# Attention scores as one product for two heads, and later first transposes in the gated feed-forward blocks

## The chip, the cores and the metric

One NeuronCore of a Trainium2 chip runs the whole program in one launch. The metric is device time in microseconds (us), the median of several runs; lower is better. TensorE is written PE, its weight loads PEld, VectorE DVE, ScalarE ACT, GpSimdE POOL, the queue that issues loads SP.

## The reference

256 tokens of width 1024 go through sixteen sublayers in float32. Eight are gated feed-forward blocks, two are squared-ReLU feed-forward blocks, the other six are mixers. Four of the mixers hold attention with heads of 64:

```python
# dsa: 8 indexer heads pick keys, then 16 heads share one key and value head
logits = jnp.einsum('bthd,bsd->bths', qi_b, ki32)
score = jnp.einsum('bth,bths->bts', wi_b, jax.nn.relu(logits))
s = jnp.einsum('bthd,btkd->bhtk', q_b, k_sel) * scale
# diff: two causal softmaxes per head, 8 heads
s = jnp.einsum('btchd,bschd->bchts', q_b, k32) * scale
a = p[:, 0] - lam_val * p[:, 1]
# pool and moba: 4 heads against 256 memory rows, no mask; moba also 12 causal heads
s = jnp.einsum('bshd,bmhd->bhsm', q, k) * (HEAD_DIM ** -0.5)
# gated feed-forward
return (jax.nn.silu(gate) * up) @ w_out
```

## The kernel before

Weights come from HBM in chunks of 1 MB (128 x 2048), through SP. Each float32 chunk is split by ACT (`hi`, L306) and DVE (`lo`, L311) into two reduced-precision parts, and each large product is issued three times (hi by hi, hi by lo, lo by hi; L528 to L530 in the gated blocks, L557 to L559 and L539 to L541 in the mixers, L598 for the down products). `take` hands the chunks out in the order of a plan that `_ffn_plan` and `_U_ORDER` write. The order of instructions on each engine is set by a scheduler that goes by priorities and by when buffers come free; each engine then runs its own list strictly in order.

**A gated feed-forward block** (`ffn`). Blocks 0 to 3 of 128 hidden columns are computed by `first` with tokens on the rows, so their results (`hts`, L728) must be turned by eight transposes (`turn`, L736) and split (L673, L674) before a down product can use them. From block 4 on the products (`u_products`, 48 for a block) give the hidden columns on the rows directly. `turn` is queued behind the 20th product of block 4, the fifth block. The first down chunk, V0, follows block 4, V1 follows block 5, and from there one down chunk follows every two blocks. `more` issues a share of the modulation sums (L1104, DVE) with each chunk in the blocks that carry them.

**Attention scores** (`softmax_pair`, and the indexer in `dsa`). Two heads of 64 are stacked on the 128 rows of `qT` and `kT`. Each head is a product of its own over its 64 rows: for query half m (128 queries) and head i, `lhsT=qT[h, 128m:...]`, `rhs=kT[h, :n]`, with n = 128 keys for m = 0 and 256 for m = 1 where the mask is causal, else 256 for both. Head i has PSUM bank a0 or a1, both halves in one bank. One such product is two MATMUL records in the trace. DVE then adds the mask and takes the row maximum (L1244, or L1246 where there is no mask), ACT takes the exponential (L1255), PE transposes (L1265) and multiplies by the values (L1280). There are 22 causal calls of `softmax_pair` (8 in dsa, 8 in diff, 6 in moba), 4 calls without mask (2 in pool, 2 in moba), and 4 pairs of indexer heads (L1351) in the form of a causal call. Keys are turned by `turn4` into the PSUM tile `tr` and copied by one ACT instruction (`to_heads`, L1202).

**Small tiles.** `square` writes a bf16 tile `junk` (one buffer), `turned` an f32 tile `turn` (two buffers). POOL does little: the root of the norms (L422, L423, in `rstd`) and a few fills.

Of the kernel before, what the change touches and what calls it, by code (L numbers as in the profile page):

```python
# [11 lines left out]
F32 = mybir.dt.float32  # L12
# [32 lines left out]
def _ffn_plan(tag, nf):  # L45
    ng = nf // 2
    out = []
    for g in range(ng):
        out += _w(tag, 2 * g, 2 * g + 1) if g < 2 else [("U", tag, 2 * g), ("U", tag, 2 * g + 1)]
        if g == 2:  # L50
            out.insert(-1, ("V", tag, 0))
        if 1 < g < ng - 3:
            out.append(("V", tag, g - 1))
    return out + [("V", tag, g) for g in range(ng - 4, ng)]
# [214 lines left out]
class _K:  # L269
# [143 lines left out]

    def square(self, src, st, n):

        j = self.tmp.tile([128, 512], BF16, name="junk")
        self.nc.scalar.activation(j, src, AF.Square, scale=1.0 / 32, accum_out=st[:, n:n + 1])  # L417

    def rstd(self, st):
# [237 lines left out]
    def turned(self, pp):  # L657

        nc = self.nc
        o = self.ps("tr")  # L660
        for m in range(2):
            t = self.tmp.tile([128, 256], F32, name="turn", bufs=2)
            nc.scalar.activation(t, pp[m], AF.Copy)
            for b in range(2):
                nc.tensor.transpose(o[:, 256 * b + 128 * m:256 * b + 128 * m + 128], t[:, 128 * b:128 * b + 128], self.ident)
        return o
# [11 lines left out]
    def ffn(self, s, act):  # L678
        nc, tc = self.nc, self.tc
        nf = 22  # L680
        with tc.tile_pool(name="hp_" + s, bufs=2) as hp:
# [59 lines left out]
            for g in range(2, 11):  # L741
                for f in (2 * g, 2 * g + 1):
                    w = self.take(("U", s, f))
                    more()
                    p = self.ps()
                    products = self.u_products(w, act, p, 1 if s[0] == "g" and f == nf - 1 else 2)
                    if f == 4:
                        self.issue(products, 20, turn)
                    else:
                        self.issue(products)  # L750
                    hidden(f, p)
                    if f == 4:
                        acc = self.new_acc()
                    if f == 4 or (f % 2 and g < 8):
                        j = 0 if f == 4 else g - 1
                        w = self.take(("V", s, j))
                        more()
                        for m in range(2):
                            self.down(m, acc[m], w, hs(j), (128, 128), j == 0, False)
# [441 lines left out]
    def to_heads(self, src, out):  # L1201
        self.nc.scalar.activation(out, self.turn4(src), AF.Copy)  # L1202

    def split_pair(self, on, oact, b0):

        pv = self.turn4(on)
        h = oact[0][:, b0:b0 + 2]
        self.nc.scalar.activation(h, pv, AF.Copy)
        self.nc.vector.tensor_tensor(oact[1][:, b0:b0 + 2], pv, h.bitcast(F32), op=OP.subtract)
# [13 lines left out]
    def softmax_pair(self, pool, qT, kT, mask, causal=True, qs=None):  # L1223


        nc = self.nc
        mx = self.tiny.tile([128, 4], F32, name="mx")
        sums = self.tiny.tile([128, 4], F32, name="sums")
        e = pool.tile([128, 2, 2, S], F32, name="e", bufs=self.ebufs)
        ns = [128 if causal else 256, 256]  # L1230
        scale = 0.125 if qs is None else 1.0
        p = [self.ps("a0"), self.ps("a1")]
        for m in range(2):
            for i in range(2):
                h = slice(64 * i, 64 * i + 64)
                o = 256 * m
                nc.tensor.matmul(p[i][:, o:o + ns[m]], lhsT=qT[h, 128 * m:128 * m + 128], rhs=kT[h, :ns[m]], start=True, stop=True)  # L1237
        for i in range(2):
            for m in range(2):
                c = 2 * m + i  # L1240
                n = ns[m]
                pi = p[i][:, 256 * m:256 * m + n]
# [72 lines left out]
    def dsa(self, act):  # L1315
        nc, tc = self.nc, self.tc
        with tc.tile_pool(name="ds", bufs=2) as dp:
# [5 lines left out]
            kk = dp.tile([128, 2, S], F32, name="kk", bufs=1)  # L1323
# [6 lines left out]
            nc.scalar.activation(kk, p.rearrange("p (j t) -> p j t", j=2), AF.Copy)  # L1330
# [11 lines left out]
            for j in range(2):  # L1342
                qT = heads(p4[1 + j])
                for b in range(2):
                    p = [self.ps("a0"), self.ps("a1")]
                    r = dp.tile([128, 2, 2, S], F32, name="e", bufs=self.ebufs)
                    for m in range(2):
                        n = 128 * (m + 1)
                        for i in range(2):
                            h = slice(64 * i, 64 * i + 64)  # L1350
                            nc.tensor.matmul(p[i][:, 256 * m:256 * m + n], lhsT=qT[h, b, 128 * m:128 * m + 128], rhs=kk[h, 1, :n],  # L1351
                                             start=True, stop=True)
                        for i in range(2):
                            nc.scalar.activation(r[:, m, i, :n], p[i][:, 256 * m:256 * m + n], AF.Relu)
# [35 lines left out]
    def diff(self, act):  # L1390
        nc, tc = self.nc, self.tc
        lam_init = 0.8 - 0.6 * math.exp(-0.3)
        with tc.tile_pool(name="df", bufs=2) as dp:
# [17 lines left out]

            chunks = lambda i: self.vprojs("diff", _U_ORDER["diff"][i], act)

            def heads(pp, name):
                q = self.evac(dp, pp, "q")
                self.rope(q.rearrange("p m (h d) -> p m h d", h=4), 4, self.rope2, 16, dp)
                qT = dp.tile([128, 2, S], F32, name=name)
                self.to_heads(q, qT)
                return qT
# [109 lines left out]
    def mem_kv(self):  # L1529

        nc = self.nc
        l, kv, pool, mact = self.mem
        kT = kv.tile([128, 2, S], F32, name="memk")
        v = kv.tile([128, 2, 256], F32, name="memv")
        k = pool.tile([128, 2, 256], F32, name="memkk")
# [7 lines left out]
        return k, kT, v  # L1543

    def mem_keys(self, k, kT):
        self.to_heads(k, kT)
        self.mem_inner.close()

    def mem_query(self, l, pool, pp, bufs=2):
        qs = self.head_scales(pool, pp, 0.125)  # L1550
# [10 lines left out]

    def pool(self, act):
        nc, tc = self.nc, self.tc
        k, kT, v = self.mem_kv()
        p4 = self.first("pool", _U_ORDER["pool"], act)
        self.mem_keys(k, kT)
        with tc.tile_pool(name="po", bufs=2) as pp:
            self.rows_ahead("pool")
            psc = [self.tmp.tile([128, 512], F32, name="upd", bufs=2) for _ in range(2)]
            nc.sync.dma_start(psc[0], self.a["pscale"][:, :512].to_broadcast([128, 512]))  # L1570
# [45 lines left out]

    def moba(self, act):
        nc, tc = self.nc, self.tc
        km, kTm, vm = self.mem_kv()
        p4 = self.first("moba", _U_ORDER["moba"][:2], act)  # L1620
        self.mem_keys(km, kTm)
        self.rows_ahead("moba")
        with tc.tile_pool(name="mb", bufs=2) as mp:
            r3 = self.tmp.tile([128, D], F32, name="xn", bufs=1)[:, :256].rearrange("p (a d) -> p a d", a=4)
            nc.sync.dma_start(r3, self.a["k_rope3"].rearrange("p (a d) -> p a d", a=4))
            tabs = {}
# [18 lines left out]
                return x, qs  # L1645

            def turned(xs, name):
                t = mp.tile([128, 2, S], F32, name=name)
                self.to_heads(xs[0], t)
                return t if xs[1] is None else (t, xs[1])  # L1650

            key = lambda pp: turned(key_x(pp), "kT")
            query = lambda pp: turned(query_x(pp), "qT")
# [108 lines left out]
```

## Time and profile before

| what | us |
|---|---|
| median of 3 runs | 2673.6 (2661.34 to 2678.39) |
| the profiled execution | 2675.0 |
| its span, first to last instruction | 2672.9 |
| PE busy | 2630.4 (98%) |
| DVE busy | 1938.7 (73%) |
| ACT busy | 1378.1 (52%) |
| POOL busy | 105.3 (4%) |

The profiled execution is 1.4 us above the median; 2.1 us of it lie outside the span. The end of a matmul is modelled in the trace, so the busy time of PE counts its pipeline's tail, and the distance between starts tells more than the duration.

### The profile page before, as it was taken

To read this page: it belongs to the slowest core of one execution; us is meant where nothing else is said; L and a number is where in the kernel's file an instruction comes from. 1 tells how busy PE (TensorE), PEld (TensorE's weight loads), DVE (VectorE), ACT (ScalarE), POOL (GpSimd) and SP (SyncE) were. 2 spreads that over 40 slices of the span, in tenths; PEclk is the share of its full clock that TensorE was granted. 3 is DMA by queue.
4 is the path that set the end of the run, shared out by engine and by line. 5 is a ranking of instruction groups with operands and counts; after the bars stand their busy time and mean duration, and the time that the engine had idled before them with its cause. 6 is when DMAs were issued, how large, how long until landed. Compare 5 with 4: busy or idle time off the path is not lost.

```text
span 2672.9 us, 43146 instructions
## 1 busy us (share of the span) xinstructions
PE 2630.4 (98%) x15984; PEld 2312.8 (87%) x15984; DVE 1938.7 (73%) x5196; ACT 1378.1 (52%) x3054; POOL 105.3 (4%) x200
## 2 busy tenths in 40 slices
PE   8999999999999999999999999999999999999999
PEld 7998789989988899899779989977899788977898
DVE  7858887587578875985868778667855776577764
ACT  5545454454554544645665454456644655465543
POOL 0004200000000000000000000000100000000000
PEclk9999999999999999999999999999999899999999
DMA  8844166476424675784538668653554545542452
GB/s 317 303 158 158 71 251 244 168 302 242 165 107 176 259 279 186 283 308 163 184 140 303 257 232 328 221 192 127 205 189 174 184 144 203 187 170 95 179 185 94
DMA packets 91156, 543.60 MB, mean 203 GB/s; under 512 B 10541, under 2 KB 11581, under 8 KB 38082
## 3 DMA queue, kind: packets, MB, share of 16 engines
q1 hardware_dynamic: 90946, 540.85, 55.1%
q8 instruction: 125, 2.05, 0.3%
q14 instruction: 85, 0.70, 0.1%
HBM read 539.69 MB, written 1.13 MB: 202 GB/s over the span
## 4 chain that ended last, share of the span: by engine, by line
PE 56%; issue 35%; DVE 5%; ACT 2%; POOL 1%; DMA 1%; SPq 0%; POOLq 0%; ACTq 0%
PE a L598 20%; PE ps L528 8%; PE ps L530 8%; PE ps L529 8%; PE a L557 2%; PE a L559 2%; PE a L558 2%; DVE y L856 2%; DVE lo L311 1%; PE a L1237 1%; PE tr L479 1%; POOL ry L423 1%; PE ps L558 1%; PE ps L557 1%; PE ps L559 1%
## 5 line engine op out<-in xcount | busy, mean ns | idle before, releaser
L311 DVE TENSOR_TENSOR lo<-raw,hi 128x256 fp32r<-128x256 f32 (+1 forms) x2964 | 1160.3, 450 | 409.2 <-ACT hi L306 408.8
L306 ACT ACTIVATE hi<-raw 128x512 fp32r<-128x512 f32 x1652 | 946.8, 624 | 792.5 <-issue 271.7
L528 PE MATMUL ps<-xh,hi 128*128 128x256 f32 x2784 | 789.3, 284 | 0.0
L530 PE MATMUL ps<-xh,lo 128*128 128x256 f32 x2784 | 789.0, 283 | 0.0
L529 PE MATMUL ps<-xl,hi 128*128 128x256 f32 x2784 | 788.4, 283 | 0.0
L529 PEld LDWEIGHTS ps<-xl,hi 128*128 128x128 f32 x2784 | 533.3, 192 | 4.1
L528 PEld LDWEIGHTS ps<-xh,hi 128*128 128x128 f32 x2784 | 533.2, 192 | 3.9
L530 PEld LDWEIGHTS ps<-xh,lo 128*128 128x128 f32 x2784 | 533.6, 192 | 0.2
L598 PE MATMUL a<-hi,hh 128*128 128x512 f32 x960 | 309.6, 396 | 0.0
L598 PE MATMUL a<-hi,hl 128*128 128x512 f32 x960 | 309.2, 396 | 0.0
L598 PE MATMUL a<-lo,hh 128*128 128x512 f32 x960 | 309.2, 396 | 0.0
L598 PEld LDWEIGHTS a<-lo,hh 128*128 128x128 f32 x960 | 179.9, 188 | 43.7
L598 PEld LDWEIGHTS a<-hi,hl 128*128 128x128 f32 x960 | 179.9, 187 | 43.5
L557 PE MATMUL a<-hi,xh 128*128 128x512 f32 x512 | 202.0, 396 | 3.4 <-ACT xh L487 1.8
L598 PEld LDWEIGHTS a<-hi,hh 128*128 128x128 f32 x960 | 173.9, 188 | 35.6 <-ACT hh L673 0.2
L559 PE MATMUL a<-hi,xl 128*128 128x512 f32 x512 | 202.4, 396 | 1.0 <-DVE xl L488 1.0
L558 PE MATMUL a<-lo,xh 128*128 128x512 f32 x512 | 200.7, 392 | 0.3 <-DVE lo L311 0.3
L1104 DVE SCALAR_TENSOR_TENSOR adaj<-adaw,cond 128x1024 bf16<-128x1024 f32 x144 | 175.8, 1221 | 34.5 <-DMA adaw<-in_ada 33.7
L557 PEld LDWEIGHTS a<-hi,xh 128*128 128x128 f32 x512 | 97.0, 189 | 26.4 <-ACT xh L492 5.2
L559 PEld LDWEIGHTS a<-hi,xl 128*128 128x128 f32 x512 | 96.6, 189 | 25.4 <-DVE xl L488 4.0
L558 PEld LDWEIGHTS a<-lo,xh 128*128 128x128 f32 x512 | 96.9, 189 | 20.6 <-DVE lo L311 0.6
L442 DVE TENSOR_TENSOR upd<-a,pg 128x512 f32<-128x512 f32 x48 | 32.9, 688 | 75.0 <-ACT junk L417 75.0
(355 smaller groups left out, 2755.7 us busy)
## 6 DMA issues: line engine op xcount, KB each, us to landing
raw<-in_wall SPq DMA_DIRECT2D x413, 1024.0 KB, 4.8
adaw<-in_ada SPq DMA_DIRECT2D x144, 512.0 KB, 6.5
G<-in_rows SPq DMA_DIRECT2D x16, 512.0 KB, 5.3
pg<-in_rows SPq DMA_DIRECT2D x12, 512.0 KB, 4.6
xn<-modd SPq DMA_DIRECT2D x12, 512.0 KB, 3.3
cond<-condd SPq DMA_DIRECT2D x7, 512.0 KB, 5.7
memt<-in_mem SPq DMA_DIRECT2D x4, 512.0 KB, 3.2
x<-in_x SPq DMA_DIRECT2D x2, 512.0 KB, 5.8
```

The costliest lines, as they stand in the source:

```text
L306: self.nc.scalar.activation(h[:, c], r[:, c], AF.Copy)
L311: self.nc.vector.tensor_tensor(l[:, c], r[:, c], h[:, c].bitcast(F32), op=OP.subtract)
L442: nc.vector.tensor_tensor(t, acc[n], pg[:, s], op=OP.mult)
L528: yield self.nc.tensor.matmul(o, lhsT=wh[:, c], rhs=xh[:, k, :], start=(k == 0), stop=False)
L529: yield self.nc.tensor.matmul(o, lhsT=wh[:, c], rhs=xl[:, k, :], start=False, stop=False)
L530: yield self.nc.tensor.matmul(o, lhsT=wl[:, c], rhs=xh[:, k, :], start=False, stop=(k == 7))
L557: yield self.nc.tensor.matmul(p, lhsT=xh[:, k, t], rhs=wh[:, c], start=(k == 0), stop=False)
L558: yield self.nc.tensor.matmul(p, lhsT=xh[:, k, t], rhs=wl[:, c], start=False, stop=False)
L559: yield self.nc.tensor.matmul(p, lhsT=xl[:, k, t], rhs=wh[:, c], start=False, stop=(k == 7))
L598: mm = lambda l, r, i, st, sp: nc.tensor.matmul(acc[i], lhsT=l[:k, t], rhs=r[:k, 1024 * b + 512 * i:1024 * b + 512 * i + 512], start=st, s ...
L856: nc.vector.scalar_tensor_tensor(c, hp[:, j, t:t + S], w(t), c, op0=OP.mult, op1=OP.add)
L1104: self.nc.vector.scalar_tensor_tensor(junk, self.ada_w.pop(n), 1.0, self.cond, op0=OP.mult, op1=OP.mult, accum_out=self.mods[k][:, c:c + 1])
```

## The change

Keys get a tile twice as wide, [128, 2, 2, 256] (`key_tile`): for each pair of heads it holds the keys of head 0 on rows 0 to 63 with zeros below, and those of head 1 on rows 64 to 127 with zeros above. POOL fills the zeros once for each tile (two fills of 64 x 512), and ACT copies keys in by two instructions of 64 rows. A score product then takes all 128 rows and gives both heads side by side, 2 x 128 or 2 x 256 columns, one query half in each of the banks a0 and a1. Six such tiles exist: one in dsa, two used in turn in diff, one in pool, two in moba (one of them first for the memory's keys). The indexer's ReLU becomes one ACT instruction for both heads. In `ffn`, `turn` comes behind the 40th product of block 4, V0 and V1 both follow block 5, and block 4 no longer calls `more`. `junk` gets two buffers, and `turned` uses it. The memory's raw keys move to another pool.

```diff
@@ _ffn_plan
         if g == 2:
-            out.insert(-1, ("V", tag, 0))
+            out.append(("V", tag, 0))
@@ ffn
-                    more()
+                    if f > 4:
+                        more()
...
                     if f == 4:
-                        self.issue(products, 20, turn)
+                        self.issue(products, 40, turn)
...
-                    if f == 4 or (f % 2 and g < 8):
-                        j = 0 if f == 4 else g - 1
+                    for j in ((0, 1) if f == 5 else (g - 1,) if f % 2 and g < 8 else ()):
@@ new
+    def key_tile(self, pool, name, tag=None):
+        t = pool.tile([128, 2, 2, S], F32, name=name, bufs=1)
+        self.nc.gpsimd.memset(t[64:, :, 0], 0.0)
+        self.nc.gpsimd.memset(t[:64, :, 1], 0.0)
+        return t
+    def to_keys(self, pv, t):
+        self.nc.scalar.activation(t[:64, :, 0], pv[:64], AF.Copy)
+        self.nc.scalar.activation(t[64:, :, 1], pv[64:], AF.Copy)
+        return t
@@ softmax_pair
+        pv = [b.rearrange("p (i s) -> p i s", i=2) for b in p]
+        for m in range(2):
+            nc.tensor.matmul(pv[m][:, :, :ns[m]], lhsT=qT[:, 128 * m:128 * m + 128], rhs=kT[:, :, :ns[m]], start=True, stop=True)
         for m in range(2):
             for i in range(2):
-                h = slice(64 * i, 64 * i + 64)
-                o = 256 * m
-                nc.tensor.matmul(p[i][:, o:o + ns[m]], lhsT=qT[h, 128 * m:128 * m + 128], rhs=kT[h, :ns[m]], start=True, stop=True)
@@ dsa, indexer
+                        nc.tensor.matmul(pv, lhsT=qT[:, b, 128 * m:128 * m + 128], rhs=kk[:, 1, :, :n], start=True, stop=True)
+                        nc.scalar.activation(r[:, m, :, :n], pv, AF.Relu)
                         for i in range(2):
-                            h = slice(64 * i, 64 * i + 64)
-                            nc.tensor.matmul(p[i][:, 256 * m:256 * m + n], lhsT=qT[h, b, 128 * m:128 * m + 128], rhs=kk[h, 1, :n],
```

On PE, the list in the dsa mixer, where scores stand between transposes and value products of other heads. `kk` are the keys, `qT` the queries, `a` the banks; before:

```order
L1237 MATMUL a_14139<-kk,qT 128x128
L1237 MATMUL a_14140<-kk,qT 128x128
L1237 MATMUL a_14139<-kk,qT 128x256
L1237 MATMUL a_14140<-kk,qT 128x256
L1280 MATMUL a_14019<-c_13684,pT 128x64 x3
L1265 MATMUL tr<-ident,e 128x128 x3
L1280 MATMUL a_14019<-c_13684,pT 128x64 x3
L1265 MATMUL tr<-ident,e 128x128 x3
L1280 MATMUL a_14019<-c_13684,pT 128x64 x3
L1197 MATMUL tr<-ident,q 128x128 x4
L1237 MATMUL a_14158<-kk,qT 128x128
L1237 MATMUL a_14158<-kk,qT 128x256
```

The same place after:

```order
L1248 MATMUL a_14122<-kk,qT 128x2x128
L1248 MATMUL a_14123<-kk,qT 128x512
L1291 MATMUL a_14002<-c_13684,pT 128x64 x3
L1276 MATMUL tr<-ident,e 128x128
L1291 MATMUL a_14002<-c_13684,pT 128x64 x3
L1276 MATMUL tr<-ident,e 128x128 x5
L1248 MATMUL a_14139<-kk,qT 128x2x128
L1291 MATMUL a_14002<-c_13684,pT 128x64 x3
```

Four products of a call became two; before, the two heads of a call stood side by side only at the first call shown, and at the second one head went alone.

On POOL, between the roots of the norms at the entry to the diff mixer (`ru`, `ry`; `sty` and `stx` are the sums of squares), a piece of the difference:

```order
 L423 TENSOR_TENSOR ry<-ru,mhalf 128x1
+L1208 MEMSET kT_19091 64x2x256
+L1209 MEMSET kT_19091 64x2x256
+L1208 MEMSET kT_19094 64x2x256
 L422 TENSOR_SCALAR ru<-sty 128x1
+L1209 MEMSET kT_19094 64x2x256
 L423 TENSOR_TENSOR ry<-ru,mhalf 128x1
```

The four fills of the two key tiles stand ahead of and between the two steps of the second token half's last root.

On PE in the first gated block, the place of the turn before:

```order
L528 MATMUL ps<-xh,hi 128x256
L529 MATMUL ps<-xl,hi 128x256
L736 MATMUL tr<-ident,hh 128x128 x4
L736 MATMUL tr<-ident,hl 128x128 x4
L530 MATMUL ps<-xh,lo 128x256
```

It stands there behind the 20th of the block's 48 products, and behind the 40th after, with no other row changed near it; the down products that read it are 28 products behind it before, and 8 and a whole block of 48 after.

## Rows read from the trace of the kernel before

**Rows 1.** The page: busy us, share of the span and instructions of each engine.
```profile
PE 2630.4 (98%) x15984; PEld 2312.8 (87%) x15984; DVE 1938.7 (73%) x5196; ACT 1378.1 (52%) x3054; POOL 105.3 (4%) x200
```

**Rows 2.** PE's waits: engine, line, waited for; total us, times, longest.
```profile
PE tr L736 <- DVE hl L728: 4.1, 4, 2.8
...
PE a L1237 <- ACT qT L1202: 0.5, 1, 0.5
```

**Rows 3.** Stretches, score products of L1237 alone: length, busy (records), clock, DMA.
```profile
1320.00:1356.00 36.00, 13.41 (x64) 7.39 (x64) 1.00 0.24 89
1786.00:1800.00 14.00, 5.04 (x16) 2.89 (x16) 0.63 0.46 164
1800.00:1850.00 50.00, 8.23 (x48) 5.25 (x48) 1.00 0.39 144
2116.00:2134.00 18.00, 8.66 (x16) 4.50 (x16) 0.53 0.25 97
2400.00:2412.00 12.00, 6.33 (x24) 3.61 (x24) 0.72 0.25 89
2412.00:2460.00 48.00, 8.78 (x40) 4.94 (x40) 1.00 0.30 110
```

**Rows 4.** The same view, indexer products of L1351 alone.
```profile
1296.00:1311.00 15.00, 7.76 (x32) 3.84 (x32) 0.78 0.55 193
```

**Rows 5.** PE in time order: start, us, line, records; a call behind projection products.
```profile
1320.15 0.39 PE L559 MATMUL ps<-hi,xl 128*128 128x512 f32 x1
1320.46 0.93 PE L1237 MATMUL a<-kk,qT 64*128 64x128 f32 x8
1321.32 0.39 PE L539 MATMUL ps<-hi,xh 128*128 128x256 f32 x1
```

**Rows 6.** The same view, one head between transposes and value products.
```profile
1348.16 0.50 PE L1265 MATMUL tr<-ident,e 128*128 128x128 f32 x3
1348.59 0.92 PE L1237 MATMUL a<-kk,qT 64*128 64x128 f32 x4
1349.43 0.88 PE L1280 MATMUL a<-c,pT 128*128 128x64 f32 x6
```

**Rows 7.** PE groups by shape: float32 products over 128 rows, 256 columns.
```profile
L848 PE MATMUL a<-hpad,taps 128*128 128x256 f32 x222 | 49.8, 380 | 2.0 <-DVE hpad L845 1.9
```

**Rows 8.** PE in time order, one such product between projection products.
```profile
257.38 0.70 PE L858 MATMUL a<-y,means 128*128 128x256 f32 x2 [1.03 <-DVE y L856]
257.73 0.47 PE L528 MATMUL ps<-xh,hi 128*128 128x256 f32 x1
258.04 0.28 PE L529 MATMUL ps<-xl,hi 128*128 128x256 f32 x1
```

**Rows 9.** Stretches, all engines PE, PEld, DVE, ACT, POOL; then PE's clock.
```profile
1335.00:1356.00 21.00, 21.00 (x134) 15.58 (x133) 14.34 (x67) 12.92 (x49) 0.00 (x0) 1.00 0.19 73
...
2116.00:2134.00 18.00, 17.48 (x47) 11.09 (x47) 13.05 (x59) 8.70 (x21) 0.25 (x2) 0.53 0.25 97
```

**Rows 10.** DVE's waits between 1321 and 1356 us.
```profile
DVE pT L1272 <- PE tr L1265: 4.5, 5, 1.4
DVE e L1244 <- PE a L1237: 2.1, 3, 1.0
```

**Rows 11.** DVE groups between 1320 and 1356 us: the mask and row maximum.
```profile
L1244 DVE CUSTOM_DVE_ANT_0 e<-a,mask 128x256 f32<-128x256 f32 x16 | 6.7, 417 | 0.0
```

**Rows 12.** ACT's key copies, by source line: ns min/median/max, first and last start.
```profile
L1202 ACT ACTIVATE kT<-tr x7: 577/597/598, 1785.3 to 2448.1; 128x512 f32<-128x512 f32 x7
```

**Rows 13.** POOL groups: the fills that exist before.
```profile
L703 POOL MEMSET hh<- 64x256 f32 x4 | 1.2, 310 | 490.9 <-PE a L598 490.9
```

**Rows 14.** POOL, DVE and PE in time order, entry to diff, second token half.
```profile
1762.72 0.47 POOL L422 TENSOR_SCALAR ru<-sty 128x1 f32<-128x1 f32 x1 [8.64 <-ACT junk L417]
...
1767.92 1.42 DVE L464 SCALAR_TENSOR_TENSOR xn<-x,ry,G 128x512 f32<-128x512 f32 x2 [0.99 <-POOL ry L423]
...
1769.66 1.03 PE L479 MATMUL tr<-ident,xn 128*128 128x128 f32 x8
```

More of the change, by code (lines that the diff above doesn't have):

```diff
@@ L414, in square @@
     def square(self, src, st, n):
-        j = self.tmp.tile([128, 512], BF16, name="junk")
+        j = self.tmp.tile([128, 512], BF16, name="junk", bufs=2)
         self.nc.scalar.activation(j, src, AF.Square, scale=1.0 / 32, accum_out=st[:, n:n + 1])
@@ L661, in turned @@
         for m in range(2):
-            t = self.tmp.tile([128, 256], F32, name="turn", bufs=2)
+            t = self.tmp.tile([128, 256], F32, name="junk", bufs=2)
             nc.scalar.activation(t, pp[m], AF.Copy)
@@ L751, in ffn @@
                     hidden(f, p)
-                    if f == 4:
+                    if f == 5:
                         acc = self.new_acc()
-                    if f == 4 or (f % 2 and g < 8):
-                        j = 0 if f == 4 else g - 1
+                    for j in ((0, 1) if f == 5 else (g - 1,) if f % 2 and g < 8 else ()):
                         w = self.take(("V", s, j))
@@ L1232, in softmax_pair @@
         p = [self.ps("a0"), self.ps("a1")]
+        pv = [b.rearrange("p (i s) -> p i s", i=2) for b in p]
+        for m in range(2):
+            nc.tensor.matmul(pv[m][:, :, :ns[m]], lhsT=qT[:, 128 * m:128 * m + 128], rhs=kT[:, :, :ns[m]], start=True, stop=True)
         for m in range(2):
             for i in range(2):
-                h = slice(64 * i, 64 * i + 64)
-                o = 256 * m
-                nc.tensor.matmul(p[i][:, o:o + ns[m]], lhsT=qT[h, 128 * m:128 * m + 128], rhs=kT[h, :ns[m]], start=True, stop=True)
-        for i in range(2):
-            for m in range(2):
                 c = 2 * m + i
                 n = ns[m]
-                pi = p[i][:, 256 * m:256 * m + n]
+                pi = pv[m][:, i, :n]
                 if mask is not None:
@@ L1322, in dsa @@
             self.rope(c0[:, :, :128].rearrange("p m (h d) -> p m h d", h=2), 2, self.rope2, 16, dp)
-            kk = dp.tile([128, 2, S], F32, name="kk", bufs=1)
+            kk = self.key_tile(dp, "kk")
             p = self.ps("tr")
@@ L1329, in dsa @@
                     nc.tensor.transpose(p[:, 256 * j + 128 * m:256 * j + 128 * m + 128], dup.rearrange("p a b -> p (a b)"), self.ident)
-            nc.scalar.activation(kk, p.rearrange("p (j t) -> p j t", j=2), AF.Copy)
+            self.to_keys(p.rearrange("p (j t) -> p j t", j=2), kk)
             wi = dp.tile([128, 2, 8], F32, name="wi", bufs=1)
@@ L1348, in dsa @@
                         n = 128 * (m + 1)
+                        pv = p[m].rearrange("p (i s) -> p i s", i=2)[:, :, :n]
+                        nc.tensor.matmul(pv, lhsT=qT[:, b, 128 * m:128 * m + 128], rhs=kk[:, 1, :, :n], start=True, stop=True)
+                        nc.scalar.activation(r[:, m, :, :n], pv, AF.Relu)
                         for i in range(2):
-                            h = slice(64 * i, 64 * i + 64)
-                            nc.tensor.matmul(p[i][:, 256 * m:256 * m + n], lhsT=qT[h, b, 128 * m:128 * m + 128], rhs=kk[h, 1, :n],
-                                             start=True, stop=True)
-                        for i in range(2):
-                            nc.scalar.activation(r[:, m, i, :n], p[i][:, 256 * m:256 * m + n], AF.Relu)
                             hd = 4 * j + 2 * b + i
@@ L1412, in diff @@
             chunks = lambda i: self.vprojs("diff", _U_ORDER["diff"][i], act)
+            keys = [self.key_tile(dp, f"kT{i}") for i in range(2)]
             def heads(pp, name):
@@ L1416, in heads @@
                 self.rope(q.rearrange("p m (h d) -> p m h d", h=4), 4, self.rope2, 16, dp)
+                if name == "kT":
+                    keys.append(keys.pop(0))
+                    return self.to_keys(self.turn4(q), keys[-1])
                 qT = dp.tile([128, 2, S], F32, name=name)
@@ L1532, in mem_kv @@
         l, kv, pool, mact = self.mem
-        kT = kv.tile([128, 2, S], F32, name="memk")
         v = kv.tile([128, 2, 256], F32, name="memv")
-        k = pool.tile([128, 2, 256], F32, name="memkk")
+        k = kv.tile([128, 2, 256], F32, name="memkk")
         pp, pv = self.vprojs(f"mem{l}", (0, 1), mact)
@@ L1542, in mem_kv, with mem_keys @@
         self.scaled(k, rs)
-        return k, kT, v
-    def mem_keys(self, k, kT):
-        self.to_heads(k, kT)
         self.mem_inner.close()
+        return k, v
+    def mem_keys(self, k, t):
+        return self.to_keys(self.turn4(k), t)
     def mem_query(self, l, pool, pp, bufs=2):
@@ L1563, in pool @@
         nc, tc = self.nc, self.tc
-        k, kT, v = self.mem_kv()
+        k, v = self.mem_kv()
         p4 = self.first("pool", _U_ORDER["pool"], act)
-        self.mem_keys(k, kT)
         with tc.tile_pool(name="po", bufs=2) as pp:
+            kT = self.mem_keys(k, self.key_tile(pp, "memk"))
             self.rows_ahead("pool")
@@ L1618, in moba @@
         nc, tc = self.nc, self.tc
-        km, kTm, vm = self.mem_kv()
+        km, vm = self.mem_kv()
         p4 = self.first("moba", _U_ORDER["moba"][:2], act)
-        self.mem_keys(km, kTm)
         self.rows_ahead("moba")
         with tc.tile_pool(name="mb", bufs=2) as mp:
+            keys = [self.key_tile(mp, f"kT{i}") for i in range(2)]
+            kTm = self.mem_keys(km, keys[1])
+            keys.insert(0, keys[0])
             r3 = self.tmp.tile([128, D], F32, name="xn", bufs=1)[:, :256].rearrange("p (a d) -> p a d", a=4)
@@ L1647, in turned @@
             def turned(xs, name):
+                if name == "kT":
+                    return self.to_keys(self.turn4(xs[0]), keys.pop(0))
                 t = mp.tile([128, 2, S], F32, name=name)
                 self.to_heads(xs[0], t)
-                return t if xs[1] is None else (t, xs[1])
+                return t, xs[1]
             key = lambda pp: turned(key_x(pp), "kT")
```

## The prediction, made before the result was known

> **What bounds the kernel now.** I read the page first, then PE's waits, then the stretches of the attention mixers, then single calls in time order. PE is busy for 98% of the span [rows 1], and its waits for other engines are small: the longest wait inside the gated blocks, for the elementwise product that `turn` needs, comes to 4.1 us in 4 places, and PE waits for copied heads ahead of a score product once, for 0.5 us [rows 2]. So the time is PE's own, and an edit is worth what it takes out of PE's list, as long as no other engine falls behind. In the mixers that has to be looked at: between 1335 and 1356 us PE is busy for 21.00 of 21.00 us and DVE for 14.34 [rows 9], and DVE waits there for PE's transposes and scores (4.5 and 2.1 us between 1321 and 1356) [rows 10]. PE leads, DVE follows with a third of its time free.
>
> **The scores before.** Between them the six stretches of [rows 3] hold 50.4 us of PE's busy time with score products and [rows 4] another 7.8 us with the indexer's, 58.2 us in all. A reader would expect two heads on separate rows to run beside each other. They do where both are issued together: eight records, a whole call, take 0.93 us [rows 5]. But where the two heads of a call are apart, four records of one head take 0.92 us [rows 6], the same time for half the work, and in the program's order most calls of dsa after the second stand so. Changing over also costs: the call of [rows 5] starts 0.31 us behind a 512-column projection product and the next product begins 0.86 us later, so it holds PE for 0.94 us where the usual step behind such a product is about 0.23 us. In [rows 6] the last of three transposes was due at about 1348.38 (steps of 0.11), PE would be free at 1348.49, and the value products begin at 1349.43: 0.94 us for one head, 1.9 us for a call. Some 55 groups of score records stand in the trace; with 0.02 to 0.2 us beyond busy time at each, the scores cost PE 59 to 69 us. I take 0.1, nearest to these two groups: 64 us.
>
> **The scores after.** No product over 128 rows with 512 float32 columns is in the trace. One with 256 columns is: 222 records of the convolution take 49.8 us [rows 7], 0.22 us each, and a product is two records, 0.44 us. I double that for 512 columns, 0.88 us; if part of a record is a fixed cost it is less, and no row gives a reason for more. Entry and exit: between projection products, a two-record product starts at 257.38 and the second projection product behind it at 258.04, 0.66 us less one usual step of 0.12, so 0.54 us [rows 8], 0.10 above its own time. Beside transposes I take no such cost. A causal call is then 0.44 + 0.88 = 1.32 us, one without mask 1.76 us. 26 causal forms (22 calls and 4 indexer pairs) and 4 without mask: 26 x 1.32 + 4 x 1.76 = 41.4 us, plus 0.10 for about half of the 60 products, 3 us: 44.4 us at the full clock. Part of it will run at 1.2 GHz, as before: granted shares of 0.63, 0.53, 0.72 [rows 3] and 0.78 [rows 4] mean that 74, 94, 56 and 44% of those stretches ran at the lower level. With 2 causal calls in the first, 2 unmasked in the second, 2 causal and 1 unmasked in the third and 4 indexer pairs in the fourth, that adds 2.0 + 3.3 + 2.5 + 2.3 = 10 us if nothing shortens there. So 44.4 to 54.5 us: against 64 the gain is 9.5 to 19.6 us. I take **14 us**, the middle, since shorter products also shorten the stretches. The ends with the unknown edges are 4.5 (59 less 54.5) and 24.6 (69 less 44.4).
>
> A rule speaks against this. The Trainium skill, TensorEngine Tiling (Array Packing), Key Properties, says that tiles of the array operate independently and can load and multiply in parallel, and under When to Use Tiling it counts a contraction of 64 as a case for two row tiles. By it two heads cost the time of one, and merging them doubles the stream. The trace agrees with it in [rows 5] and shows in [rows 6] that the order seldom makes use of it.
>
> **Does the gain reach the end?** PE is what DVE and ACT wait for in these stretches [rows 9, 10]. Taking about 4 us of the 36 in dsa leaves DVE some slack, so I let the gain through whole.
>
> **The key tiles.** Keys need two ACT copies for one, each of 512 columns at 0.597 us [rows 12]; a copy of half the rows is no shorter by any row, so 10 copies add 6 us to ACT, which is 52% busy. What shows is where PE waits for the first keys of a mixer, 0.5 us before [rows 2]; 0.6 us more in one or two mixers is **+1 us**, at most +2.5 if all four show it. Fills: twelve of 64 x 512; one of half that length takes 0.31 us [rows 13], so 0.31 to 0.62 us each, and 0.55 as an estimate from it. They sit on POOL, 4% busy, in the shade of other work, with one exception. At the entry to diff three stand ahead of `ru` of the second token half, and one between it and `ry`. They wait for the last product of the block ahead, at about 1760.4, so the three end at about 1762.1, ahead of the 1762.72 at which `ru` starts; the fourth delays `ry` by about 0.5 us. Behind it are DVE's `xn`, done at 1769.34, and PE's transposes at 1769.66 [rows 14]: 0.32 us of slack, so PE may lose 0.2 us. I put that at nothing. The wider ReLU of the indexer, `junk` with two buffers and the memory keys' pool change nothing that PE waits for.
>
> **The gated blocks.** `turn` moves back by 20 products of 0.12 us, 2.4 us. Of the four waits, 4.1 us in sum, the longest of 2.8 keeps 0.4 and the others (1.3 us between three) go [rows 2]: 3.7 us at most. The later V0 keeps 56 products, 6.7 us, to split two groups; the split was never waited for with 28. DVE's modulation sums start a chunk later, which helps. If what made DVE late is a late weight chunk, PE meets it a little further on; I take **-3 us**, bounds 0 and -4.
>
> **Sum.** -14 + 1 - 3 = -16 us against the profiled execution's 2675.0, 2659.0. That execution lies 1.4 us above the median, so **2658 us** (2657.6).
>
> **Rivals.**
> *The clock stays up.* The stretch of 18 us in the pool mixer runs at 0.53, almost wholly at 1.2 GHz, while half of PE's time there goes to 64-row products [rows 3, 9]. If full-height products bring the 2.4 GHz level back early, the scores gain 19.6, and the other work of the slow stretches runs faster too: of 17.48 us in pool 8.8 are not scores and would halve, -4.4, and about as much in the others together. -19.6 - 9 + 1 - 3: 2644 against the execution, with some slack lost 2646. Against it: waits of PE come ahead of these stretches and stay, and a stretch with many of the same products, [rows 6], runs at the full clock [rows 9].
> *DVE or ACT takes over.* DVE is 68% busy in [rows 9]; where calls follow each other closely, each needs two row maxima of 0.417 and two shorter ones on DVE, with weight splits between. If three quarters of the gain turn into waits, -4 + 1 - 2: 2669.
> *A wait that stands in PE's way.* Each 512-column product needs a whole bank that DVE reads last in the call ahead, two maxima of 0.417 us [rows 11], and everything behind it in PE's list waits too; before, a head could go as soon as its own bank was free. At 1 us for each of 30 such products the cost is 30 us against a gain of 16: 2687. The point from which it decides is 0.53 us for each. Before, this wait is near zero because the list was filled with projection products; dsa's last third and moba have few left.
> *Concurrency lost.* If most calls ran side by side as in [rows 5], merging would cost 1.32 + 0.1 against 0.94 each, 30 x 0.48 = 14 us on top: 2687 as well. It needs more than two calls in three to run so; [rows 3] speaks against it, with 13.41 us for the 8 calls of dsa, 1.7 each.
>
> **Chances.** Forecast 0.52 (2648 to 2667), clock 0.22 (2638 to 2652), DVE or ACT 0.16 (2664 to 2674), the wait 0.07, concurrency 0.03. The range, 2640 to 2674, leaves out the last two and the far ends of the clock case. One per cent, about what a measurement of this kernel can tell from no change, is 27 us: faster by that lies below 2647, half of the clock case and the forecast's far tail, 0.2; slower by that, above 2700, is a part of the last two, 0.04; the rest, 0.76, is within.
>
> **What would show it.** In the changed profile, score products should come in groups of two records, 0.22 us apart for 256 columns and 0.44 for 512, with 45 to 55 us of PE busy time in place of 58. PE's wait for `hl` at the turn should fall below 1 us in sum. DVE's wait for scores should shrink; if PE's wait for row maxima (L1244's line) or for freed banks grows past 10 us, the third rival holds. A granted clock near 1 in the pool mixer would prove the first. I am wrong if a 512-column record takes clearly more than 0.44 us, or if the gain in PE's list shows up again as idle time there.

## The result, and the profile after

The changed kernel takes 2644.5 us (median of 8 executions, 2642.3 to 2651.4), the kernel before 2670.3 on the same chip (8 executions, 2660.0 to 2678.4): ratio 0.991 with an interval of 0.989 to 0.993, 25.7 us less by the medians. The forecast was 2658, the range 2640 to 2674. The profiled execution takes 2643.9 us, its span 2642.1.

The page of the changed kernel, busy us, share of the span and instructions of each engine, and PE's granted clock in 40 slices:

```profile
PE 2601.1 (98%) x15864; PEld 2297.5 (87%) x15864; DVE 1936.6 (73%) x5196; ACT 1381.3 (52%) x3056; POOL 113.2 (4%) x212
...
PEclk9999899999999999999999999999999999999999
```

PE still fills the span, with 29 us less busy time than in [rows 1]; the other engines do what they did. So the time came out of PE's list, and nothing else took over. PE's groups of the changed kernel by shape, those of score products:

```profile
L1248 PE MATMUL a<-kT,qT 128*128 128x512 f32 x36 | 18.7, 605 | 0.5 <-DVE mx L1255 0.5
...
L1248 PE MATMUL a<-kT,qT 128*128 128x256 f32 x28 | 8.8, 396 | 1.5 <-ACT qT L1202 1.4
...
L1361 PE MATMUL a<-kk,qT 128*128 128x512 f32 x8 | 4.2, 610 | 0.0
...
L1361 PE MATMUL a<-kk,qT 128*128 128x256 f32 x8 | 2.7, 420 | 0.0
```

A record of 512 columns is 0.21 us longer than one of 256, as the step of 0.22 us in [rows 7] said. All 120 score records keep PE busy for 49.5 us, against 58.2 us of 240 records before [rows 3, 4]; both figures count the tail behind each group. PE's waits in the changed kernel (engine, line, waited for; total us, times, longest):

```profile
PE tr L1197 <- ACT kT L1214: 1.5, 1, 1.5
PE a L1248 <- ACT qT L1202: 1.4, 1, 1.4
...
PE a L1248 <- ACT memk L1214: 0.5, 1, 0.5
PE a L1248 <- DVE mx L1255: 0.5, 1, 0.5
```

The wait for `hl` of [rows 2] is gone. PE waits for key copies instead (1.5 and 0.5 us), for the first copied queries of diff (`qT`, 1.4 us) and for a row maximum once, 0.5 us.

Then the clock. The pool mixer of the changed kernel, two stretches (length; busy us and records of PE, PEld, DVE, ACT and POOL; PE's granted clock):

```profile
2088.00:2110.00 22.00, 19.32 (x106) 14.80 (x105) 21.60 (x76) 18.46 (x43) 0.25 (x2) 1.00 0.40 144
2110.00:2130.00 20.00, 19.32 (x111) 16.74 (x110) 10.15 (x26) 4.39 (x10) 0.00 (x0) 1.00 0.31 106
```

Where [rows 9] showed 0.53, it is 1.00 throughout. Between 1276 and 2490 us, where the four attention mixers lie, the profile before has 47.8 us at the lower of the two levels (1.2 GHz) and the profile after 6.8 us. Each is one execution, and the one before, with a mean clock of 0.989, is one of its kernel's slower ones: the profile of e6 below, with the old scores and a mean clock of 0.994, has 13.7 us there. Measured from the update of x that ends a stage to that which ends the next, diff is 8.4 us shorter, pool 8.0, dsa 5.0, moba 3.5, and four of the gated blocks 0.8, 3.3, 1.0 and 1.1; the other eight stages differ by at most 1.4 us either way.

The mean clock differs from one execution of a kernel to the next, and the time with it: 23 executions of the kernel before, on one chip, go from 2679 us at 0.988 to 2659 at 0.996, on average 2.2 us for each 0.001. So each run below has its mean clock beside it.

### The profile page after: what moved, and what is told of

Same layout as the page of the kernel before. It is cut to its first block, busy times and chain, and to the rows that moved or that the text cites. A ratio compares the mean times of both kernels' runs of the same rounds, so it can differ in the third digit from the quotient of the medians.

```text
span 2642.1 us, 42944 instructions
## 1 busy us (share of the span) xinstructions
PE 2601.1 (98%) x15864; PEld 2297.5 (87%) x15864; DVE 1936.6 (73%) x5196; ACT 1381.3 (52%) x3056; POOL 113.2 (4%) x212
## 4 chain that ended last, share of the span: by engine, by line
PE 57%; issue 34%; DVE 6%; ACT 2%; POOL 1%; DMA 0%; SPq 0%; POOLq 0%; ACTq 0%; DVEq 0%
PE a L598 20%; PE ps L528 8%; PE ps L530 8%; PE ps L529 8%; PE a L557 3%; PE a L559 3%; PE a L558 2%; DVE y L856 2%; DVE lo L311 2%; PE tr L479 1%; POOL ry L423 1%; ACT junk L417 1%; ACT hi L306 1%; DMA raw<-in_wall 0%; PE a L848 0%
## 5 line engine op out<-in xcount | busy, mean ns | idle before, releaser
L598 PEld LDWEIGHTS a<-lo,hh 128*128 128x128 f32 x960 | 180.2, 188 | 43.5
L711 ACT ACTIVATE hh<-h 128x256 fp32r<-128x256 f32 x144 | 59.1, 411 | 80.8 <-DVE h L710 80.7
```

What stands on the lines that cost most here:

```text
L598: mm = lambda l, r, i, st, sp: nc.tensor.matmul(acc[i], lhsT=l[:k, t], rhs=r[:k, 1024 * b + 512 * i:1024 * b + 512 * i + 512], start=st, s ...
L711: nc.scalar.activation(hh[:n, b], h[:n], AF.Copy)
```

## The experiments

Each run is compared with executions of the kernel before on its own chip. Two theories stood at the start. The **rows theory**: products over 64 rows hold the granted clock down, and the gain is the clock's. The **merging theory**: the gain is that of 60 products in place of 120, with fewer entries and exits. A third, the **turn theory**, put most of the gain to the gated blocks. The later runs look at what is left of these.

| run | median us | ratio (95%) | mean clock |
|---|---|---|---|
| before (the 29 executions beside e5 to e8) | 2669.9 | | 0.992 |
| changed | 2644.5 | 0.991 (0.989, 0.993) | 0.996 |
| e1 gated blocks alone | 2664.9 | 0.998 (0.997, 1.000) | 0.993 |
| e2 scores alone | 2652.7 | 0.993 (0.991, 0.996) | 0.996 |
| e3 full height, a product per head | 2653.1 | 0.994 (0.992, 0.996) | 0.994 |
| e4 the same, half height | 2669.2 | 1.000 (0.998, 1.002) | 0.991 |
| e5 heads side by side, before | 2673.4 | 1.002 (1.000, 1.003) | 0.992 |
| e6 later V0 alone, before | 2666.1 | 0.999 (0.997, 1.002) | 0.993 |
| e7 changed, half height | 2670.5 | 1.001 (0.999, 1.003) | 0.991 |
| e8 changed, no zeros | 2643.3 | 0.991 (0.989, 0.994) | 0.996 |
| e9 changed, V0 as before | 2654.8 | 0.993 (0.991, 0.995) | 0.995 |
| e10 changed, wide bias | 2643.1 | 0.989 (0.987, 0.991) | 0.997 |
| e11 changed, scores twice | 2687.4 | 1.008 (1.006, 1.010) | 0.995 |
| e12 the same, half height | 2711.1 | 1.016 (1.013, 1.019) | 0.991 |

**e1 and e2: the two parts alone.** e1 is the kernel before with the hunks of `_ffn_plan` and `ffn` alone; e2 is the changed kernel without them.

```diff
-                        self.issue(products, 20, turn)
+                        self.issue(products, 40, turn)
```

> The kernel before with the change in the gated blocks alone (turn behind the 40th product, V0 behind block 5, no modulation step with block 4); attention as before. Rows theory (the gain of the attention part is that products over 64 rows, mostly alone, went out of PE's list): the gated blocks give 4 to 7 us, as the stage ends of the two traces say, so about 2665 against 2670. Turn theory (the gated blocks carry most of the gain): 12 us or more, 2658 or less.

> The changed kernel with the gated blocks put back as they were before. Rows theory: 19 to 23 us faster than before, about 2650, the clock at its upper level in diff, pool and moba as in the changed kernel. Turn theory: 13 us or less, 2657 or more.

By the ratios the gated blocks alone give 4.5 us, which is not clear of nothing (at most 9), and the scores alone 18 (11 to 25); by the medians it is 2 and 14.5. The turn theory falls: most of the gain is in the mixers.

**e3 and e4: the height alone.** Both keep the changed kernel's key tiles and gated blocks, and give each head its own bank and its own products, as before. e3 runs them over 128 rows, e4 over 64; nothing else differs. From e3 to e4, the line of `softmax_pair` (the indexer's goes the same way):

```diff
-                nc.tensor.matmul(pv[i][:, m, :ns[m]], lhsT=qT[:, 128 * m:128 * m + 128], rhs=kT[:, i, :ns[m]], start=True, stop=True)
+                h = slice(64 * i, 64 * i + 64)
+                nc.tensor.matmul(pv[i][:, m, :ns[m]], lhsT=qT[h, 128 * m:128 * m + 128], rhs=kT[h, i, :ns[m]], start=True, stop=True)
```

> The changed kernel with its zero-filled keys, but each head a product of its own over all 128 rows (four products for a call, one bank for each head, as before the change). The columns that PE streams are those of the changed kernel, the number of score instructions is that before. Rows theory: within 4 us of the changed kernel, 2642 to 2649, clock up. Merging theory (what counts is that two heads are one instruction, so fewer instructions, waits and a better order): 10 us or more slower than the changed kernel, 2655 or more.

> The same as the full-rows kernel in everything (key tiles, fills, two key copies, turn behind the 40th product, order of the code), but each product over its head's 64 rows alone, as before the change. Rows theory: the attention gain is gone, 18 to 24 us slower than the changed kernel, 2663 to 2669, and the stretches at 1.2 GHz in dsa, diff, pool and moba are back. Merging theory: the same time as the full-rows kernel within 3 us.

Half height loses 16 us, and with them the whole gain. The pool mixer of e3 and then that of e4, same columns as above:

```profile
2108.00:2122.00 14.00, 13.31 (x99) 12.19 (x99) 12.14 (x32) 6.22 (x16) 0.00 (x0) 1.00 0.38 129
```

```profile
2108.00:2121.50 13.50, 13.39 (x33) 8.40 (x34) 9.59 (x42) 6.91 (x16) 0.25 (x2) 0.50 0.14 58
```

The stretch at half clock is back with the 64 rows, and PE gets through 33 records there; in dsa, where the expectation had one too, this execution has none. e3 in turn is 8.6 us slower than the changed kernel by the medians, between what the two theories gave it. Its clock is 0.0016 lower (some 4 us by the slope above) and PE waits 2.7 us more in all (40.0 against 37.3; among it 3.7 us for `xh` in moba, where the changed kernel waits 0.2); the rest of 2 us is within the spread. By the medians merging is thus the smaller part of the gain; whether the clock and the wait of e3 come of the products' number or of the order that the list took, no run shows.

**e5: the two heads of a call side by side in the kernel before.** A fixed order of issue (head 1 ahead of head 0) keeps the 64-row products of a call together.

```diff
-            for i in range(2):
+            for i in (1, 0):
...
+                with (self.tc.issue_after(last.ins) if last else ExitStack()):
```

> The kernel before, with the four products of a call put in a fixed order, head 1 ahead of head 0, so that the two 64-row heads always stand together in PE's list; nothing else is changed. Concurrency theory (two row tiles side by side do the work of one, and what cost time before was only that the heads stood apart): 30 calls at about 1 us in place of 64 us, so PE's score time near 30 to 35 us and a time of 2640 to 2650, as good as the changed kernel or better. Rows theory (64-row products keep the granted clock low, wherever they stand): the score time falls, but the mean clock stays at 0.990 to 0.993, and the time is 2652 to 2664. If the chip gains nothing from pairs, 2666 as before.

Nothing is gained: 2673 us against 2670, the third of the expected cases. PE's busy time with scores falls to 45.2 us (52.1 in e6, which has the order before at a similar clock, 0.994 against 0.993), but the number of score groups in PE's list (runs of score records with no other product between) does not (56, 55 before), nor does the mean clock move.

**e7 and e8: the changed kernel with half the rows, and without the zeros.** The first edit is e7's (the indexer's line goes the same way), the second e8's.

```diff
-            nc.tensor.matmul(pv[m][:, :, :ns[m]], lhsT=qT[:, 128 * m:128 * m + 128], rhs=kT[:, :, :ns[m]], start=True, stop=True)
+            nc.tensor.matmul(pv[m][:, :, :ns[m]], lhsT=qT[:64, 128 * m:128 * m + 128], rhs=kT[:64, :, :ns[m]], start=True, stop=True)
```

```diff
-        self.nc.scalar.activation(t[:64, :, 0], pv[:64], AF.Copy)
-        self.nc.scalar.activation(t[64:, :, 1], pv[64:], AF.Copy)
+        self.nc.scalar.activation(t[:, :, 0], pv, AF.Copy)
+        self.nc.scalar.activation(t[:, :, 1], pv, AF.Copy)
```

> The changed kernel with its 60 merged products over rows 0 to 63 alone (it leaves out head 1, whose scores become zero); number, columns and order of the products stay as in the changed kernel. Rows theory (the number of rows at work sets the granted clock): mean clock 0.990 to 0.994 and 2651 to 2664, with half-clock stretches back in the pool and diff mixers. Merging theory (fewer and longer products, whatever their rows, do it): clock 0.995 to 0.997 and 2642 to 2650, as the changed kernel.

> The changed kernel with both key copies filled with the keys of both heads in place of zeros, so that each score is the sum over both heads (the scores are no longer those of single heads); each ACT copy has 128 rows in place of 64. Rows theory by shape alone: the same clock (0.995 to 0.997) and 2642 to 2650. If the zeros matter (half of the operands at work, a clock that depends on data), the clock moves by 0.002 or more and the time by 4 us or more with it. If an ACT copy of half the rows is cheaper than one of all, PE's waits for the first keys grow from 1.5 us and the time rises by 1 to 3 us.

Cutting the rows costs 26 us, more than the rows theory gave, and undoes the whole change, though products and columns are those of the changed kernel, and so is PE's order but for seven records in dsa; filling the zeros with keys changes nothing. The merging theory, which gave e7 the changed kernel's time, falls. The same 20.5 us of dsa, in e7 and then in e8:

```profile
1294.00:1314.50 20.50, 20.50 (x40) 9.92 (x39) 11.67 (x36) 8.62 (x18) 0.00 (x0) 0.50 0.28 100
```

```profile
1294.00:1314.50 20.50, 19.53 (x88) 14.46 (x88) 20.35 (x88) 12.18 (x28) 0.00 (x0) 1.00 0.23 93
```

The pool mixer, where the expectation had a stretch at half clock too, runs at full clock in this execution of e7, 64 rows or not:

```profile
2105.00:2125.00 20.00, 18.23 (x86) 12.49 (x85) 19.59 (x72) 16.62 (x36) 0.26 (x2) 1.00 0.43 159
```

So a single stretch in a single execution tells little of a kernel; the mean clock over its executions does.

The clock isn't all of it. At equal mean clock (0.996) an execution of e7 takes 2656.7 us and the median of three of the changed kernel 2643.8. Where that comes from shows in PE's time order at the full clock (start, us, line, records). First the changed kernel, then e7, the same place in moba, six transposes, a product of 256 columns, the value products:

```profile
2422.11 0.83 PE L1276 MATMUL tr<-ident,e 128*128 128x128 f32 x6
2422.78 0.60 PE L1248 MATMUL a<-kT,qT 128*128 128x256 f32 x2
2423.21 0.42 PE L1291 MATMUL a<-v,pT 128*128 128x64 f32 x2
```

```profile
2448.22 0.82 PE L1276 MATMUL tr<-ident,e 128*128 128x128 f32 x6
2448.98 0.70 PE L1248 MATMUL a<-kT,qT 64*128 64x256 f32 x2
2449.60 0.43 PE L1291 MATMUL a<-v,pT 128*128 128x64 f32 x2
```

From the transposes to the score 0.67 us against 0.76, from the score to the values 0.43 against 0.62. So going from 128 rows to 64 costs 0.09 us and coming back 0.19, 0.28 us for a group, in time that no wait of the list names. The entry of 0.20 us behind a transpose, against 0.11, stands the same in nearly all groups of e7, e4 and the kernel before that run at the full clock. With 44 groups in e7 that is 12.3 us, and 2656.7, a single execution, less 2643.8 is 12.9. The Trainium skill, TensorEngine Tiling (Array Packing), Key Properties, says that changing the tiling mode drains TensorE. These steps agree with it, and show what a change there and back costs here.

**e11 and e12: twice the time at 64 rows, as many changes.** That left the question whether the time at 64 rows lowers the clock or the changes do. Each score product is done twice in a row, over 128 rows in e11 (its edit in `softmax_pair` is shown), over 64 in e12.

```diff
-            nc.tensor.matmul(pv[m][:, :, :ns[m]], lhsT=qT[:, 128 * m:128 * m + 128], rhs=kT[:, :, :ns[m]], start=True, stop=True)
+            for _ in range(2):
+                nc.tensor.matmul(pv[m][:, :, :ns[m]], lhsT=qT[:, 128 * m:128 * m + 128], rhs=kT[:, :, :ns[m]], start=True, stop=True)
```

> The changed kernel with each of its 60 score products done twice in a row into the same place. By the steps of the trace (0.43 and 0.86 us for a product) a call without the causal saving is 1.72 us and a causal one 1.29 us, so 26 x 1.29 + 4 x 1.72 = 40.4 us more if PE takes them whole: 2680 to 2690 with the clock at 0.995 to 0.997. Less than that means that part of a score product lies in time that PE loses anyway.

> The same with the 60 doubled products over rows 0 to 63 alone (head 1's scores left out, as in the half-height run before). The time at 64 rows doubles, the number of changes between 64 and 128 rows stays near 44. Rows theory (time at 64 rows lowers the clock): the distance to the full-height twin grows from 26 us to 36 us or more, 2718 to 2735, with a mean clock of 0.984 to 0.989. Change-over theory (PE's stops at the changes lower the clock and cost 0.29 us each): the distance stays at 20 to 28 us, 2702 to 2713, with a mean clock of 0.990 to 0.993.

e11 adds 42.8 us to the changed kernel, near the 40.4 from the steps, so PE takes scores at 0.43 us for 256 columns and 0.86 for 512, and no part of them is free. e12 lies 23.8 us above e11, some 10 us more or less by the two intervals, where e7 lay 26.0 above the changed kernel; the 36 us or more of the rows theory are outside. Its mean clock is 0.991, that of e7, though single executions of e12 go from 0.985 to 0.996. The one at 0.996 takes 2697.6 us, 11.5 above the median of the three of e11 at that clock (2686.1), and 46 groups at 0.28 us are 12.9. So twice the time at 64 rows adds no loss that shows, and the groups are 46 and 44. The rows theory, as I had put it, falls too: the loss doesn't grow with the time at 64 rows. That the steps' part goes with the number of changes between 64 and 128 rows follows from the 0.28 us for a group. That the clock's part does is what is left, but isn't shown: no run varied that number alone, and e1 and e6 with 55 groups have a mean clock of 0.993, e7 with 44 one of 0.991.

**e6 and e9: which half of the gated-block part.** e6 is the kernel before with the later V0 and splits, the turn at 20; e9 the changed kernel with the turn at 40, V0 and splits as before.

```diff
-            out.insert(-1, ("V", tag, 0))
+            out.append(("V", tag, 0))
```

> The kernel before with the later V0 and the later splits of the gated blocks alone; the transposes of the turn stay behind the 20th product. If the 4.5 us that the gated-block part gained are the turn's place (the wait for hl), nothing goes: 2665 to 2670, ratio 0.999 to 1.002, and the wait for hl stays near 4 us. If they come from the order of V0 and the splits, the same gain as the whole part: 2660 to 2665, ratio 0.997 to 0.999.

> The changed kernel with the order of V0 and of the splits as before; the turn's transposes stay behind the 40th product. If the place of the turn is what the gated-block part is worth, nothing is lost: 2642 to 2648, and PE waits less than 1 us for hl. If the later V0 and splits carry it, or are needed with the later turn, some of the 8 us that the whole part is worth beside the new scores come back: 2649 to 2654.

Neither half shows a gain: e6 is not clear of the kernel before, and e9 is where e2 is, the changed kernel without this part (both 0.993). PE's wait at the turn in e6, and the wait that stands in its place in e9:

```profile
PE tr L736 <- DVE hl L728: 3.8, 3, 2.5
```

```profile
PE a L598 <- DVE hl L674: 4.1, 6, 1.4
```

With V0 late and the turn early PE waits for `hl` as before. With the turn late and V0 early only 8 of block 4's 48 products lie between the turn and V0, and V0's products wait for the split instead. Both together have neither wait.

**e10: another place with few rows.** The convolution's bias goes over 1 row, right where every profile has 10 us at half clock.

```diff
-            ones = cp.tile([1, 128], F32R, name="ones", bufs=1)
+            ones = cp.tile([128, 128], F32R, name="ones", bufs=1)
...
+                nc.gpsimd.memset(t.bitcast(F32), 0.0)
```

> The changed kernel with another place of few rows widened: the 8 products of the convolution's bias, over 1 row before, go over 128 rows, of which 127 are zero. They stand at the start of the half-clock stretch of 10.2 us that every profile has at about 315. Rows theory beyond the scores: that stretch shortens by 3 us or more or goes, and the time is 2638 to 2643. If products of one column and PE's wait of 2.6 us behind them are what holds the clock there, the stretch stays at 10.2 us and the time at 2643 to 2648.

The stretch stays as it was, 10.2 us:

```profile
314.40:324.60 10.20, 7.57 (x20) 5.74 (x20) 7.86 (x19) 6.48 (x12) 0.72 (x1) 0.50 0.28 104
```

So the few rows of the bias don't hold it. Products of one column and PE's wait of 2.6 us for `xh` are left as candidates; no run shows whether it is one of them. The median is 2643.1 us, but on a chip where the kernel before took 2675.3; it is not shown to be faster than the changed kernel.

## Why the prediction was right, and where it was off

**The bound.** That PE's own list sets the time held: PE is 98% busy before and after, and its waits are 38.8 us in all before and 37.3 after. e5 is the exception: some 7 us less busy time with scores, and the time did not fall.

**The scores after.** 0.44 us for 256 columns and 0.88 for 512 were the forecast, 0.43 and 0.86 are the steps, and e11 confirms their sum. 49.5 us busy lie within the 45 to 55, and DVE's waits for scores fall from 11.7 us to 4.8, as the signs said.

**The term that was mis-sized** is that of the scores, 14 us, at both of its ends. For the old scores I took 0.1 us beyond busy time at each of some 55 groups, "nearest to these two groups", but the two groups give 0.94 us against 0.93 and 0.92 busy [rows 5, 6], 0.01 and 0.02. The group of e7 shown above gives 0.02 too: six transposes at 0.11 us end at 2448.88, the values begin at 2449.60, 0.72 us later, and it is busy for 0.70. With 0.02 the old scores cost 59 us, not 64; the price of the change of height lies inside that busy time. For the new scores I took 50 us, with 5 us of half clock in it, where e11 prices the same products at 42.8. So the old were taken 5 us too high and the new 7 too high, which cancels in part. By e2 the scores and key tiles gave 18 us (11 to 25), by its medians 14.5, where 13 was the forecast.

What the sum put at nothing is the other work at half clock. Between the two profiled executions 41 of 47.8 us at the lower level went away; their mean clocks, 0.989 and 0.996, are some 15 us apart by the slope of 2.2 us for each 0.001.

**The rival that came true** in part is "the clock stays up", with its 2644 to 2646 us, to which I gave a chance of 0.22; the measured 2644.5 is below the 2648 where the forecast's own band ends, and the range held it because it took that rival in. That full height keeps the clock up is shown (e3 against e4, e8 against e7). Its mechanism, that PE's time at 64 rows holds the clock down, does not survive e12. The pool mixer at 1.00 is the sign that it named, and a weak one, since e7 shows it too.

At equal mean clock of 0.996 the changed kernel is 16.5 us below the kernel before (2643.8, three executions, against 2660.3, six executions on two other chips). The other 7 to 9 us of the gain are the 0.003 to 0.004 of clock by the slope. That 16.5 is so near the forecast's 16 is in part luck: two executions of e2 at that clock lie at 2651.5 on average, so scores and key tiles give some 9 us there, where I had 13, and the gated blocks beside them some 8, where I had 3.

**The key tiles**, +1 us. The 0.5 us that I took from [rows 2] as PE's wait for the first keys is its wait for the first copied queries of diff, `qT`, which come behind the keys on ACT. PE's waits for keys are 1.5, 0.5 and 0.2 us after, one of 0.3 before. That wait for `qT` is 1.4 us after, with one more copy of 0.57 us ahead of it on ACT; but it is 3.2 us in e6, with a single key copy, where ACT waited for a weight chunk, so it isn't the key tiles' alone. As forecast, a copy of 64 rows is no shorter: 0.592 to 0.597 us (L1214), against 0.577 to 0.598 for 128 rows before. The fills take 0.52 us each, estimated at 0.55. At the entry to diff the fourth stands where it was expected, ahead of `ry`:

```profile
1751.27 0.40 POOL L422 TENSOR_SCALAR ru<-sty 128x1 f32<-128x1 f32 x1 [0.52 <-ACT junk L417]
1751.73 0.52 POOL L1209 MEMSET kT<- 64x512 f32 x1
1752.22 0.56 POOL L423 TENSOR_TENSOR ry<-ru,mhalf 128x1 f32<-128x1 f32 x1
```

PE waits for `xn` at that place in neither profile, so the delay cost nothing. By the medians of e4 and e1 the key tiles and their second copies cost 4 us, with intervals of some 5 us on each side, which settles no more than that they are cheap.

**The gated blocks**, -3 us: -2 by the medians alone (e1, not clear of nothing), -5 to -8 beside the new scores (e2 against the changed kernel, by ratios and by medians). The wait for `hl` went as forecast. The later turn takes it away, and the later V0 keeps it from coming back as a wait for the split: in e9, with 8 products between turn and V0, that wait is 4.1 us.

**The other rivals** did not come. The wait for row maxima is 0.5 us, where 10 would have been the sign. DVE and ACT follow, since PE's waits did not grow. Lost concurrency shows no price in the whole kernel: with the heads always side by side (e5), the kernel before gains nothing.

**Open:** why the 7 us of busy time that e5 takes from the scores don't show in its time (PE's waits in its profile are 44.5 us in all against 38.8 before, but 43.5 in e6 without that edit); why half-clock stretches fall in other places from one execution to the next; and what lowers the clock in kernels with 64-row products, the changes of height or something that comes with them. An order of the kernel before with few changes of height (several calls in a row) wasn't tried, because each call waits for the softmax of the one ahead.

## What to carry to other kernels

A product over half the rows between products over all of them has a price of its own, 0.28 us here for going there and back, and the kernels with such groups ran at a lower mean clock as well; padding the keys with zeros to full height was the cheaper way, though it doubled the columns of each product. Count the groups at half height in PE's list: twice the products in as many groups cost no more on top than once (e12 against e11, e7 against the changed kernel). When a step in a list is moved later to hide a wait, look at who reads its result: a move of the reader may be what makes it pay.

## What the runs showed of the hardware that was not expected

- 64-row products between 128-row ones: first product 0.20 us behind the last transpose in place of 0.11, next 128-row product 0.19 us later than behind a full-height one (e7 against the changed kernel, at the full clock). The cost appears in no wait.
- The mean clock goes with the height: 0.991 to 0.993 in all kernels with 64-row scores, 0.994 to 0.997 in all with full-height ones, with keys or with zeros in the other half (0.996 and 0.996), and 0.991 with the time at 64 rows once or twice (e7, e12).
- Two heads on separate halves of the array, side by side (e5), shorten PE's busy time with scores by some 7 us and the kernel not at all.
